# Half of an RWKV layer's operand steps made beside its recurrence instead of ahead of it

## The chip, the cores and the metric

The kernel runs on one core of one Trainium2 chip. The metric is the time of one launch in device microseconds, the median of several runs. A core has the engines PE (matrix multiply, with weight loads shown apart as PEld), DVE (vector), ACT (scalar functions), POOL (general purpose) and SP, whose queue issues every DMA of this kernel. All engines work on SBUF, 128 partitions wide; matrix products land in PSUM.

## The reference: what is computed

One inference step of a two-layer trunk over 1152 tokens (128 context tokens and 1024 latent tokens), width 1024. Layer 0 is attention, layer 1 a bidirectional RWKV-7 mixer with 16 heads of 64; each layer ends with an MLP. The change lies wholly in the RWKV mixer:

```
def rwkv_mixer(h, p, s0):
    xx = token_shift_centred(h)
    xr, xw, xk, xv, xa, xg = (h + xx * mu[n] for n in range(6))
    r = (xr @ w_rkv[0]).reshape(hs)
    k = (xk @ w_rkv[1]).reshape(hs)
    v = (xv @ w_rkv[2]).reshape(hs)
    g = jax.nn.sigmoid(xg @ g1) @ g2
    kk = (k * k_k).astype(F32)
    kk = kk * lax.rsqrt(jnp.sum(kk * kk, axis=-1, keepdims=True) + 1e-12)
    for d in range(2):
        wlog = -jax.nn.softplus(-(w0[d] + jnp.tanh(xw @ w1[d]) @ w2[d])) - 0.5
        decay = jnp.exp(-jnp.exp(wlog.astype(F32))).reshape(hs)
        a = jax.nn.sigmoid(a0[d] + (xa @ a1[d]) @ a2[d]).reshape(hs)
        kd = k * (1.0 + (a - 1.0) * k_a)
        y, sf = wkv_scan(r, decay, kd, v, kk, a, s0[:, d], reverse=(d == 1))
        bonuses.append(jnp.sum(r * kd * r_k, axis=-1, keepdims=True) * v)
...
def step(S, inp):
    r_t, w_t, k_t, v_t, kk_t, kka_t = inp
    sk = jnp.einsum('bhvk,bhk->bhv', S, kk_t)
    S = S * w_t[:, :, None, :] - sk[..., None] * kka_t[:, :, None, :] + v_t[..., None] * k_t[:, :, None, :]
    return S, jnp.einsum('bhvk,bhk->bhv', S, r_t)
```

The sum of both directions is normalised per head, the bonuses are added, the gate g is multiplied in, and w_o follows.

## The kernel before, in words

The mixer has two functions. `rwkv_proj` makes everything that is a product of the whole layer; `rwkv_scan` runs the recurrence in chunks of 64 tokens, 18 chunks per sequence, for eight pairs of heads, both directions at once.

**Projections.** The activations lie as features by tokens in three blocks of 384 columns. `lowranks` makes the first low-rank products; `dense` then runs the three dense products k, r and v, each as 8 output tiles by 3 token blocks with three matmuls per weight piece (the values are split in a high and a low half), at line 1111, from weights that `load_piece` and the halving at 1098 and 1099 (POOL for the low half `pwl`) prepare. The token mixes of the next product are made beside it (1064 to 1068).

Beside the dense products r and v, a generator `operands` (line 1243) is stepped. One operand step is one head pair and one token block, 24 in all, and makes what the recurrence reads, for each direction: two second low-rank products (`second`, line 1189, three matmuls of halves each), tanh and exponentials on ACT, a prefix sum on DVE (1277), the products `ar` (kk and r times the decays, POOL, 1285 and 1286) and `bk` (1290 on POOL, 1291 and 1293 on DVE, 1294 on POOL), stored to DRAM as `ard` and `bkd`, and the triangular products `ng` of the 32-token halves (PE, 1305, masked by DVE at 1307). At its end come the bonus terms (1313 on POOL, 1314 on DVE, `head_sums` at 1124). Its working tiles come from pool `rp2`, and, once the inputs of the dense products are used up, from the activations' pool (`etiles`). The loop steps it at every second iteration from the fifth on, so that all 24 steps are done when the projections end. The triangular matrices of a pair are inverted by `invert` (31 rounds of two DVE operations, 1364 and 1365): for the first three pairs behind their last operand step, for the others in the scan. The first two chunks of all pairs are inverted together in one run of 128 partitions.

**Pools.** When `rwkv_proj` returns, its pools (`rp1`, `rp2`, the activations and two in PSUM) are dropped and the pools of the scan take the space. A tile of the scan can so exist only once the tiles of the projections that lay there are done.

**Scan.** `rwkv_scan` builds a plan: `put` gives each generator a number of steps spread over a stretch of time units (one unit is one recurrence step), and the sorted list is the order in which instructions are emitted. A scheduler then orders each engine's instructions from a simulated timeline. The generators are `invert`; `prepare` (1428), which loads `ar`, `bk` and the triangles for six chunks, forms the chunk products `gp` (1467, one matmul of 128 weight columns by 192 columns for each head and chunk) and masks them into `g` (DVE, 1468), and joins the inverses `tt` with two small products (1483 and 1489); `recurrence` (1497), 18 steps per pair and 144 in all; and `finish` (1600), which normalises the output of a pair with tiles from a ring "f". One recurrence step on PE is `cp` (1542), then x = -cp on ACT (1550), the product of x and the inverse (1557), its copy to `mu` on ACT (1559), and the new state (1564), to which DVE adds `sd` (1567), the decayed state, that POOL makes (1548) from the state before. The outputs `yp` (1554 and 1573) run beside it.

Every operand of these PE products is written at an own `tile_position`, so that heads of 64 use halves or quarters of the array.

Of the kernel before, what the change touches and what calls it, by code (L numbers as in the profile page):

```python
# [10 lines left out]
F32 = mybir.dt.float32  # L11
# [10 lines left out]
KD = 8  # L22
# [27 lines left out]
NEK = 1  # L50
# [39 lines left out]
class Net:  # L90
# [930 lines left out]
    def rwkv_proj(self, act, early, pool, pse, ps):  # L1021
        A, S, V, G, T, dma, dr = self.A, self.S, self.V, self.G, self.T, self.dma, self.dr
        KE = (V, G)[KDE]
# [21 lines left out]
        hb = early.tile([128, 120], F32, name="hb")  # L1045
# [7 lines left out]
        vs, turn = [], 0  # L1053
# [30 lines left out]
        def load_piece(srcs):  # L1084
            raw = early.tile([128, KD, 128], F32, tag="praw", name=self.nm("praw"), bufs=1)
# [28 lines left out]
        def out32(dst, b, p):  # L1114
            o = pool.tile([128, TB], F32, tag="ro", name=self.nm("ro"), bufs=2)
# [4 lines left out]
        def head_sums(x, out):  # L1120

            sp = ps.tile([128, 3, 2], F32, tag="st", name=self.nm("hst"), bufs=1)
# [4 lines left out]
        def rows_out(out, src):  # L1127

            o, x = out.rearrange("k e (t p) -> (k e t) p", p=128), src.rearrange("p k e t -> p (k e t)")
            for i in range(0, x.shape[1], 72):  # L1130
                tp = pse.tile([128, HW], F32, tag="tp", name=self.nm("rtp"), bufs=3)[0:72, 0:128]
                T.transpose(tp, x[:, i : i + 72], self.ident)
                rt = load(None, "rt")[0:72, 0:128]
                S.copy(rt, tp)
                dma(o[i : i + 72], rt)

        def lowranks(n, hs, after):
# [12 lines left out]
            for b in range(3):  # L1150
                t = early.tile([128, TB], F32, tag="mix", name=self.nm("lt"), bufs=3)
# [10 lines left out]
                if n == 5:  # L1162
                    x = pool.tile([128, 2, TB], F32R, tag=("ar", "ar", "bk")[b], name=self.nm("lg"), bufs=2)
                    hi, lo = x[:, 0], x[:, 1]
                else:
                    hi = pool.tile([128, TB], F32R, tag="lth", name=self.nm("lth"), bufs=6)
                    lo = pool.tile([128, TB], F32R, tag="ltl", name=self.nm("ltl"), bufs=6)
                S.copy(hi, t)
                V.tensor_tensor(lo, t, f32(hi), op=ALU.subtract)
                tl[n, b] = (hi, lo)  # L1170
                after(b)

        def second_weights(n, p8):

            raw = pool.tile([128, 128], F32, tag="w2r", name=self.nm("w2r"), bufs=1)
            src = A[{1: "rwkv_w2", 4: "rwkv_a2", 5: "rwkv_g2"}[n]][0]
            dma(raw, (src if n == 5 else src.rearrange("d r n -> (d r) n"))[:, p8 * 128 : p8 * 128 + 128])
            hi = pool.tile([128, 128], F32R, tag="w2hi", name=self.nm("w2hi"), bufs=3)
            lo = pool.tile([128, 128], F32R, tag="w2lo", name=self.nm("w2lo"), bufs=3)
            S.copy(hi, raw)  # L1180
            V.tensor_tensor(lo, raw, f32(hi), op=ALU.subtract)
            return hi, lo

        def second(n, w, b, r):
            hi, lo = w
            th, tlo = tl[n, b]
            p = pse.tile([128, HW], F32, tag="lp", name=self.nm("lp"), bufs=3)[:, 0:TB]
            for j, (x, y) in enumerate(((hi, th), (hi, tlo), (lo, th))):
                T.matmul(p, x[r], y[r], start=j == 0, stop=j == 2)
# [27 lines left out]
        def v_done(p8, b, p):  # L1217
            o = out32(self.vd[:, p8], b, p)
            for c in range(0, 6, 3):
# [3 lines left out]
                vt = early.tile([128, TB], F32, tag="mix", name=self.nm("vt"), bufs=3)[0:64]  # L1223
# [669 lines left out]
```

## Time and profile before

| | us |
|---|---|
| median of three runs | 4447.08 |
| lowest and highest run | 4445.78 and 4457.35 |
| the profiled execution, device time | 4456.37 |
| its span in the trace | 4454.5 |
| busy PE, DVE, ACT, POOL in it | 3996.6, 2783.2, 1681.4, 1227.4 |

The profile is of one execution. "Busy" is the time in which an engine executes; what it waits for is inferred from semaphore events. A stage of the kernel can be told apart by cutting the span at the times at which a line first and last runs: the dense products (line 1111) end at 2710.6, the recurrence's x (line 1550) runs from 2790.8 to 3483.8, so the RWKV mixer's second half of projections and its scan fill about 2262 to 3490. Rows in the windows view give, for each stretch, the busy time of each engine with the number of instructions, then the clock that PE was granted as a share of full speed, the DMA share and GB/s.

### The profile page before, as it was taken

Reading aid. Unit: us, or ns where it says so; the run is one execution under the profiler, and the core shown is the slowest. Engines: PE = TensorE matmul, PEld = TensorE weight load, DVE = VectorE, ACT = ScalarE, POOL = GpSimd, SP = SyncE. Lnnn points to the kernel's source line nnn. Section 1 sums busy time; section 2 is a strip of 40 time slices with the busy share of each in tenths; the row PEclk is TensorE's granted clock in tenths of the full one; section 3 lists DMA queues with packets and bytes.
Section 4 is the critical chain, followed back from the end, with each engine's and each line's share of the span. In section 5 each row is a group of like instructions: output and inputs, shape, how many; then the busy total and the mean of one; then the engine's idle time right before and its main releaser. Section 6 shows DMA issues by size and latency. Waiting matters only on the chain. (4 is left out here: it accounts for less than half of the span.)

```text
span 4454.5 us, 76517 instructions
## 1 busy us (share of the span) xinstructions
PE 3996.6 (90%) x29026; PEld 3437.9 (77%) x29026; DVE 2783.2 (62%) x5866; ACT 1681.4 (38%) x3930; POOL 1227.4 (28%) x1519
## 2 busy tenths in 40 slices
PE   7989998879999999988976786989999699999998
PEld 5767776658888888868976675777777589999997
DVE  6856778865666676675248785767543564444445
ACT  5436776544211211143444453444444242222112
POOL 1223557650000000024255575434443200000001
PEclk8999999889999999989987786999999699999999
DMA  4444223232222222221334667765653511111112
GB/s 163 128 141 117 76 73 90 81 103 96 72 72 69 78 72 72 86 91 34 108 116 136 176 206 182 156 152 136 155 135 87 183 62 48 38 48 43 43 38 99
DMA packets 651182, 452.22 MB, mean 102 GB/s; under 512 B 301894, under 2 KB 606526, under 8 KB 649662
## 3 DMA queue, kind: packets, MB, share of 16 engines
q1 hardware_dynamic: 650816, 447.33, 34.9%
q8 instruction: 230, 3.77, 0.4%
q14 instruction: 136, 1.11, 0.1%
HBM read 323.45 MB, written 123.76 MB: 100 GB/s over the span
## 5 line engine op out<-in xcount | busy, mean ns | idle before, releaser
L956 PE MATMUL acc<-w2h,f 128*128 128x512 f32 x2304 | 733.7, 392 | 7.6 <-ACT f L835 5.1
L936 PE MATMUL mp<-h_b,w1h 128*128 128x384 f32 x1536 | 521.8, 340 | 0.0
L936 PE MATMUL mp<-h_a,w1h 128*128 128x384 f32 x1536 | 517.0, 337 | 0.8 <-ACT h L300 0.7
L936 PE MATMUL mp<-h_a,w1l 128*128 128x384 f32 x1536 | 517.0, 337 | 0.0
L956 PEld LDWEIGHTS acc<-w2h,f 128*128 128x128 f32 x2304 | 431.9, 188 | 104.5 <-ACT f L835 6.8
L956 PE MATMUL acc<-w2l,f 128*128 128x512 f32 x1152 | 451.3, 392 | 0.0
L962 DVE TENSOR_TENSOR acc<-acc,acc 128x1024 f32<-128x1024 f32 x270 | 329.0, 1219 | 135.5 <-PE acc L956 132.9
L660 POOL TENSOR_TENSOR ptl<-pt,pth 128x512 fp32r<-128x512 f32 x192 | 248.0, 1294 | 215.9 <-DVE pth L659 126.2
L936 PEld LDWEIGHTS mp<-h_a,w1h 128*128 128x128 f32 x1536 | 288.5, 188 | 7.0 <-issue 2.0
L936 PEld LDWEIGHTS mp<-h_b,w1h 128*128 128x128 f32 x1536 | 288.9, 188 | 4.2 <-issue 0.7
L1467 PE MATMUL gp<-ar,bk 128*128 128x192 f32 x1152 | 278.7, 372 | 14.8 <-DMA bk<-bkd 10.2
L936 PEld LDWEIGHTS mp<-h_a,w1l 128*128 128x128 f32 x1536 | 289.1, 188 | 0.1
L1111 PE MATMUL rp<-mxh,pwh 128*128 128x384 f32 (+2 forms) x720 | 267.3, 372 | 24.3 <-ACT lt L1154 7.1
L938 ACT ACTIVATE mt<-mp 128x384 f32<-128x384 f32 x192 | 94.0, 490 | 493.3 <-PE mp L936 491.6
L1111 PE MATMUL rp<-h_b,pwh 128*128 128x384 f32 (+2 forms) x720 | 263.5, 366 | 2.0 <-DVE h_b L1068 2.0
L988 POOL TENSOR_TENSOR acc<-acc,mraw 128x1024 f32<-128x1024 f32 x6 | 15.3, 2558 | 900.9 <-DVE mrv L110 894.2
L1111 PE MATMUL rp<-mxh,pwl 128*128 128x384 f32 (+2 forms) x720 | 261.9, 365 | 0.0
L956 PEld LDWEIGHTS acc<-w2l,f 128*128 128x128 f32 x1152 | 216.2, 188 | 44.7 <-issue 3.1
L1793 POOL MEMSET h_a<- 128x8 f32 x4 | 0.3, 113 | 904.3 <-PE mp L936 904.3
L940 DVE TENSOR_TENSOR mf<-mt 128x384 f32<-128x384 f32 x192 | 106.4, 554 | 212.4 <-ACT mt L938 212.3
L1468 DVE TENSOR_TENSOR g<-gp,gm 128x384 f32<-128x384 f32 x288 | 156.8, 555 | 109.9 <-PE gp L1467 98.6
L1467 PEld LDWEIGHTS gp<-ar,bk 128*128 128x128 f32 x1152 | 197.1, 204 | 31.7 <-POOL ar L1444 10.4
(452 smaller groups left out, 9584.0 us busy)
## 6 DMA issues: line engine op xcount, KB each, us to landing
mraw<-in_mlp_w_dram SPq DMA_DIRECT2D x64, 1024.0 KB
adaw<-in_w_ada_dram SPq DMA_DIRECT2D x80, 512.0 KB
bkd<-bk SPq DMA_DIRECT2D x48, 384.0 KB
ard<-ar SPq DMA_DIRECT2D x48, 384.0 KB
q<-QSd SPq DMA_DIRECT2D x256, 64.0 KB
ar<-ard SPq DMA_DIRECT2D x40, 384.0 KB
praw<-in_rwkv_w_rkv_dram SPq DMA_DIRECT2D x24, 512.0 KB
x1d<-acc SPq DMA_DIRECT2D x18, 512.0 KB
```

Of the source, the lines that this page charges most:

```text
L660: (V if w < 4 else G).tensor_tensor(c["l"][:, g : g + w, o], t["tp", g][:, 0:w], f32(c["h"][:, g : g + w, o]), op=ALU.subtract)
L936: T.matmul(p, x[:, k, :], act[b].v[y][:, k], start=k == 0 and i == 0, stop=k == KD - 1 and i == 2)
L938: S.activation(t, p, AF.Relu)
L940: V.tensor_tensor(f, t, t, op=ALU.mult)
L956: T.matmul(p[:, hf], x[:, cols], y[:, n], start=j == 0 and i == 0, stop=j == 1 and i == 2)
L962: V.tensor_tensor(a, a, pf, op=ALU.add)
L988: (G if b < 2 else V).tensor_tensor(a, a, x1[t], op=ALU.add)
L1111: T.matmul(p, x[:, k, :], a[y][:, k], start=k == 0 and i == 0, stop=k == KD - 1 and i == 2)
L1467: T.matmul(gp[:, j], x, ar[:, q + j].rearrange("p a t -> p (a t)"), start=True, stop=True)
L1468: V.tensor_tensor(g[:, e].rearrange("p j a t -> p j (a t)"), gp, gm[:, d, e, None].to_broadcast([128, 2, 192]), op=ALU.mult)
L1793: net.G.memset(a.hx[:, :, z : z + 1], 0.0)
```

## The change

The operand steps of the last four pairs leave the projections. The loop now steps `operands` at twelve listed iterations only, and `rwkv_proj` returns the generator; the scan's plan steps it for the other twelve, three for each pair, from 10 units ahead of the first recurrence step on and 24 units per pair. For this the pool `rp2` and the pool of late tiles stay open through both stages, and the operand tiles come from `rp2` alone (ten "e" tiles; `ar` and `bk` share three). A table `banks` says from which PSUM tag the operand steps take their tiles, and the scan changes it to its own tags.

```
-EB, LB, KDE, OF, BKE = 7, 4, 1, 5, 1
-PL = 13
+EB, LB, ABE, OF = 10, 4, 3, (7, 10, 13, 16, 19, 26, 29, 32, 35, 38, 42, 46)
+PL = 9
-GB = 8
-AB = 3
-GT = 22
+GB = 6
+AB = 2
+FB = 3
+GT = 18
-TTB = 5
+TTB = 4
-PI = 3
+PI = 2
+PO = 4
...
-            if i >= OF and i % 2:
+            if i in OF:
                 next(ops)
-        for _ in ops:
-            pass
-        rows_out(self.bsd, bss)
+        return ops
...
+        def made(n):
+            for _ in range(n):
+                next(ops)
+                yield
...
-        put(self.invert(pool, KD), 32, -12, 8)
+        put(self.invert(KD), 32, -6, 8)
+        put(self.invert(KD + 1), 32, 103.5, 116.5)
...
+            if p >= PO:
+                put(made(3), 3, 24 * (p - PO) - 10, 24 * (p - PO) + 14)
             if p >= PI:
-                put(self.invert(pool, p), 32, t - 45, t - 25)
+                put(self.invert(p), 32, t - 45, t - 32)
             for b in range(3):
-                put(prepare(p, b, us[p]), 16, t + 18 * b - PL, t + 18 * b - PL + 9)
+                put(prepare(p, b, us[p]), 16, t + 18 * b - PL, t + 18 * b - PL + 7)
```

Beside both stages' tiles in SBUF, rings are shorter (above: `rp`, `ar`, `g`, `tt`; the finish's "f" ring falls from five tiles to three, `sd` from two to one), prepare leads by 9 units instead of 13, the inverses of the first chunks are split in two runs of 64 partitions (four pairs each), and `tt` is 64 columns wide instead of 128. The x of a recurrence step is therefore written per head by two ACT operations into fixed tiles:

```
-                x = pool.tile([128, 2, 64], F32, tag=f"x{k}", name=self.nm("x"), bufs=1)
-                S.mul(x, cp[:, 0], -1.0)
+                x = xts[k]
+                for e in range(2):
+                    S.mul(x[row(e), e], cp[row(e), 0], -1.0)
```

The chunk products are made in two tiles of 64 weight columns, at positions (0, 0) and (0, 64):

```
-                            x = bk[e][:, q + j].rearrange("p a t -> p (a t)")
-                            T.matmul(gp[:, j], x, ar[:, q + j].rearrange("p a t -> p (a t)"), start=True, stop=True)
+                            for x in range(2):
+                                T.matmul(gp[row(x), j].rearrange("p (a t) -> p a t", t=64), bk[e][:, x, q + j], ar[:, :, q + j], start=True, stop=True, tile_position=(0, 64 * x))
```

The second low-rank products become one fp32 matmul each in place of three of halves, and the halves of the low-rank activations and weights are no longer made:

```
-            for j, (x, y) in enumerate(((hi, th), (hi, tlo), (lo, th))):
-                T.matmul(p, x[r], y[r], start=j == 0, stop=j == 2)
+            T.matmul(p, w[r], tl[n, b][r], start=True, stop=True)
```

Last, the arrays `ard`, `bkd` and `vtd` in DRAM and their tiles put the pair's two members ahead of the chunks, so that a row of one member's six chunks is 1536 bytes in one piece:

```
-        self.vtd = dr.tile([KD, 64, NC, 2, 64], F32, name="vtd")
-        self.ard = [dr.tile([KD, 128, NC, 2, 64], F32, name=f"ard{d}") for d in range(2)]
-        self.bkd = [dr.tile([KD, 128, NC, 2, 64], F32, name=f"bkd{d}") for d in range(2)]
+        self.vtd = dr.tile([KD, 64, 2, NC, 64], F32, name="vtd")
+        self.ard = [dr.tile([KD, 128, 2, NC, 64], F32, name=f"ard{d}") for d in range(2)]
+        self.bkd = [dr.tile([KD, 128, 2, NC, 64], F32, name=f"bkd{d}") for d in range(2)]
```

The first place where instructions move is PE at the seam between projections and scan. Before (lp are the second low-rank products, ng the triangles and hst the bonus sums of operand steps, rtp the transposed bonus sums, gp the first chunk product of the scan):

```order
L1305 MATMUL ng_27131<-ar_27120,bk_27127 32x32 x24
L1305 MATMUL ng_27190<-bk_27186,ar_27178 32x32 x24
L1124 MATMUL hst_27220<-ones_19676,es_27103 128x2 x3
L1305 MATMUL ng_27260<-ar_27249,bk_27256 32x32 x24
L1305 MATMUL ng_27315<-bk_27311,ar_27304 32x32 x24
L1124 MATMUL hst_27344<-ones_19676,es_27232 128x2 x3
L1132 MATMUL rtp_27354<-ident,bss 72x128
L1467 MATMUL gp_27445<-ar_27431,bk_27387 128x192 x2
```

After, at the same place (rp is the last dense product, vp its transposes, sp the first state of the recurrence, yp its first outputs):

```order
L1118 MATMUL rp_25438<-mxh_23357,pwl_25136 128x384
L1215 MATMUL vp_25466<-ident,ro_25463 64x128 x3
L1215 MATMUL vp_25473<-ident,ro_25463 64x128 x3
L1182 MATMUL lp_25558<-lt_19897,w_5009_25544 128x384
L1182 MATMUL lp_25564<-lt_20104,w_5010_25546 128x384
L1182 MATMUL lp_25616<-lt_19897,w_5009_25544 128x384
L1182 MATMUL lp_25622<-lt_20104,w_5010_25546 128x384
L1517 MATMUL sp_26032<-ident,s_5106_26029 128x64 x2
L1545 MATMUL yp_26042<-rp_25512,mu_26035 64x64
L1291 MATMUL ng_25584<-ar_25571,bk_25579 32x32 x24
```

Before, the last operand steps stood behind the last dense product; after, the thirteenth step stands among the first instructions of the scan.

The second place is POOL in the scan's first part, between the recurrence's `sd` products. Before (g is a copy into the chunk products' tile, ar with ey a decay diagonal of prepare):

```order
L1548 TENSOR_TENSOR sd_29016<-mu_28388,Dc 64x128 x2
L1494 COPY g_28986<-ar_28973 64x2x64 x2
L1494 COPY g_29021<-ar_28973 64x2x64 x2
L1494 COPY g_29056<-ar_28973 64x2x64 x2
L1548 TENSOR_TENSOR sd_28625<-mu_28074,Dc 64x128 x2
L1444 TENSOR_TENSOR ar_29493<-ey,Dc 128x6x64
L1548 TENSOR_TENSOR sd_29140<-mu_29084,Dc 64x128 x2
```

After (the products ar, kd and bk of 128x384 belong to a made operand step):

```order
L1538 TENSOR_TENSOR sd_27406<-mu_27278,Dc 64x128 x2
L1271 TENSOR_TENSOR ar_27434<-kk_27413,ec_27418 128x384
L1272 TENSOR_TENSOR ar_27434<-r_27415,ec_27418 128x384
L1276 TENSOR_TENSOR kd_27438<-kd_27438,k_27411 128x384
L1538 TENSOR_TENSOR sd_27665<-mu_27278,Dc 64x128 x2
L1260 MEMSET ec_27474 128x6
L1280 TENSOR_TENSOR bk_27442<-kd_27438,en_27430 128x384
L1271 TENSOR_TENSOR ar_27490<-kk_27413,ec_27474 128x384
L1272 TENSOR_TENSOR ar_27490<-r_27415,ec_27474 128x384
L1276 TENSOR_TENSOR kd_27494<-kd_27494,k_27411 128x384
L1280 TENSOR_TENSOR bk_27498<-kd_27494,en_27486 128x384
```

Here three to six products of an operand step stand between one `sd` and the next (the last row is followed by one more, at 1299, and then by the next `sd`), where small copies stood. In the whole order, the thirteenth step's first products stand right behind the last dense one, and the twenty-fourth step is done when 45 of the 144 recurrence steps have been issued.

More of the change, by code (lines that the diff above doesn't have):

```diff
@@ L1052, in rwkv_proj, with bank @@
         tl = {}
-        vs, turn = [], 0
+        vs = []
+        self.banks = dict(tp=(pse, "tp", 3), lp=(pse, "lp", 3), st=(ps, "st", 1), ng=(ps, "ng", 1))
+        def bank(what, shape):
+            p, tag, bufs = self.banks[what]
+            return p.tile(shape, F32, tag=tag, name=self.nm(what), bufs=bufs)
         def mix(n, b):
@@ L1120, in head_sums @@
         def head_sums(x, out):
-            sp = ps.tile([128, 3, 2], F32, tag="st", name=self.nm("hst"), bufs=1)
+            sp = bank("st", [128, 3, 2])
             for t in range(3):
@@ L1129, in rows_out @@
             o, x = out.rearrange("k e (t p) -> (k e t) p", p=128), src.rearrange("p k e t -> p (k e t)")
[L1130 to L1133, printed above, removed]
+            n = min(x.shape[1], 72)
+            for i in range(0, x.shape[1], n):
+                tp = bank("tp", [128, HW])[0:n, 0:128]
+                T.transpose(tp, x[:, i : i + n], self.ident)
+                rt = load(None, "rt")[0:n, 0:128]
                 S.copy(rt, tp)
-                dma(o[i : i + 72], rt)
+                dma(o[i : i + n], rt)
         def lowranks(n, hs, after):
@@ L1161, in lowranks @@
                     V.tensor_scalar(t, t, 0.5, 0.5, op0=ALU.mult, op1=ALU.add)
[L1162 to L1170, printed above, removed]
+                tl[n, b] = t
                 after(b)
         def second_weights(n, p8):
-            raw = pool.tile([128, 128], F32, tag="w2r", name=self.nm("w2r"), bufs=1)
+            w = pool.tile([128, 128], F32, tag="w2", name=self.nm("w2"), bufs=3)
             src = A[{1: "rwkv_w2", 4: "rwkv_a2", 5: "rwkv_g2"}[n]][0]
[L1177 to L1182, printed above, removed]
-        def second(n, w, b, r):
-            hi, lo = w
-            th, tlo = tl[n, b]
-            p = pse.tile([128, HW], F32, tag="lp", name=self.nm("lp"), bufs=3)[:, 0:TB]
-            for j, (x, y) in enumerate(((hi, th), (hi, tlo), (lo, th))):
-                T.matmul(p, x[r], y[r], start=j == 0, stop=j == 2)
+            dma(w, (src if n == 5 else src.rearrange("d r n -> (d r) n"))[:, p8 * 128 : p8 * 128 + 128])
+            return w
+        def second(n, w, b, r):
+            p = bank("lp", [128, HW])[:, 0:TB]
+            T.matmul(p, w[r], tl[n, b][r], start=True, stop=True)
             return p
@@ L1251, in operands @@
             self.tri = {}
-            ndp = self.tri[KD] = dr.tile([KD, 2, 2, 2, 2, 32, 32], F32, name="ndp")
+            for i in range(2):
+                self.tri[KD + i] = dr.tile([KD // 2, 2, 2, 2, 2, 32, 32], F32, name=f"ndp{i}")
             for p8 in range(KD):
@@ L1317, in operands @@
                         self.tri[p8] = nd
+                        rows_out(self.bsd[p8 : p8 + 1], bss[:, p8 : p8 + 1])
                         if p8 < PI:
-                            for _ in self.invert(pool, p8):
+                            for _ in self.invert(p8):
                                 pass
@@ L1387, in rwkv_scan @@
         row = lambda e: slice(64 * e, 64 * e + 64)
-        bks = [[pool.tile([128, NB, 2, 64], F32, name=f"bk{i}{e}") for e in range(2)] for i in range(2)]
+        bks = [[pool.tile([128, 2, NB, 64], F32, name=f"bk{i}{e}") for e in range(2)] for i in range(2)]
         for i in range(2):
@@ L1807, in body @@
         P.drop("tacc", "tm", "traw", "tpt")
-        pool, ps = P.add("rp2"), P.add("rpp2", "right", PSUM)
-        net.rwkv_proj(hs, early, pool, pse, ps)
-        P.drop("rp2", "rp1", "act", "rpp1", "rpp2")
-        late, psl = P.add("scl", "right"), P.add("scpl", "right", PSUM)
+        late, ps = P.add("scl", "right"), P.add("rpp2", "right", PSUM)
+        net.inv_pool = P.add("rp2", "right")
+        ops = net.rwkv_proj(hs, early, net.inv_pool, late, pse, ps)
+        P.drop("rp1", "act", "rpp1", "rpp2")
+        psl = P.add("scpl", "right", PSUM)
         pool, ps = P.add("sc"), P.add("scp", space=PSUM)
-        last = net.rwkv_scan(pool, late, ps, psl)
-        P.drop("sc", "scp")
+        last = net.rwkv_scan(pool, late, ps, psl, ops)
+        P.drop("sc", "scp", "rp2")
         net.act_pool = P.add("act")
```

125 lines of the change are left out of this document (60 added, 65 removed).

## Prediction

> **What bounds the kernel now.** I read the windows view first, cut at the stages of the odd layer: the second half of the projections (2262 to 2755), the start of the scan, the scan's first 46 recurrence steps, and the rest. Columns: stretch, length, busy us of PE, PEld, DVE, ACT, POOL, clock, DMA share, GB/s.
>
> ```profile
> 2262.00:2755.00 493.00, 373.40 (x3964) 328.86 (x3963) 339.19 (x507) 227.67 (x505) 294.97 (x297) 0.80 0.57 171
> 2755.00:2790.00 35.00, 22.34 (x162) 17.36 (x162) 21.90 (x55) 5.79 (x18) 15.70 (x32) 0.60 1.02 179
> 2790.00:3030.00 240.00, 223.81 (x3209) 180.97 (x3209) 164.46 (x443) 108.14 (x339) 96.25 (x234) 0.95 0.70 149
> 3030.00:3490.00 460.00, 414.27 (x6049) 333.97 (x6050) 222.79 (x589) 189.91 (x619) 182.35 (x421) 0.89 0.51 123
> 2262.00:2350.00 88.00, 81.02 (x691) 74.61 (x691) 29.75 (x38) 29.78 (x63) 43.63 (x41) 0.91 0.51 150
> ```
>
> The scan is PE's: 93% in its first part, 90% in the rest. The projections are PE's while few operand steps run (81 of 88 us, 92%), but over their second half PE is busy only 76%. The sources of the last dense product and of the recurrence's x place the seam, and the length of the whole:
>
> ```profile
> span 4454.5 us, 76517 instructions
> L1111 PE MATMUL rp<-mxh,pwl x720: 332/338/687, 1983.2 to 2710.6; 128*128 128x384 f32 x144, 128*128 128x386 f32 x24, 128*128 128x388 f32 x12
> L1550 ACT ACTIVATE x<-cp x144: 262/278/295, 2790.8 to 3483.8; 128x128 f32<-128x128 f32 x144
> ```
>
> From 2711 to 2791 neither dense product nor recurrence runs. What holds the second half is seen in the timeline of DVE and POOL (start, duration, line):
>
> ```profile
> 2727.20 0.55 DVE L1291 SCALAR_TENSOR_TENSOR es<-es,kk 128x384 f32<-128x384 f32 x1
> 2727.66 0.61 DVE L1314 SCALAR_TENSOR_TENSOR es<-r,CB,es 128x384 f32<-128x384 f32 x1
> 2728.19 0.97 DVE L1277 TENSOR_TENSOR_SCAN es<-m,es 128x390 f32<-128x390 f32 x1
> 2733.63 1.04 DVE L1291 SCALAR_TENSOR_TENSOR tha<-tha,kk 128x384 f32<-128x384 f32 x1 [2.19 <-ACT kd L1289]
> ```
>
> ```profile
> 2721.87 1.00 POOL L1290 TENSOR_TENSOR es<-es,k 128x384 f32<-128x384 f32 x1 [0.46 <-ACT es L1289]
> 2732.47 0.92 POOL L1286 TENSOR_TENSOR ar<-r,es 128x384 f32<-128x384 f32 x1
> 2734.20 1.26 POOL L1286 TENSOR_TENSOR ar<-r,ec 128x384 f32<-128x384 f32 x1
> 2748.75 0.85 POOL L1294 TENSOR_TENSOR bk<-es 128x384 f32<-128x384 f32 x1
> 2749.58 0.98 POOL L1313 TENSOR_TENSOR es<-es,es 128x384 f32<-128x384 f32 x1
> ```
>
> L1291 takes 0.55 while POOL is idle and 1.04 beside a POOL operation; L1286 takes 0.92 alone and 1.26 beside DVE. So I count the two engines as taking turns. One operand step, alone: DVE 2 x (0.97 + 0.55 + 0.55, the last taken for L1293 as for L1291) + 2 x 0.61 (L1314, and the product kk at L1262 taken like it) = 5.4; POOL 2 x (0.92 + 0.92 + 1.00 + 0.85) + 0.98 = 8.4; together 13.8 us. The groups of the projections' second half, and below them two of the scan's first part, give the other work of this kind (busy, mean ns):
>
> ```profile
> L1365 DVE TENSOR_TENSOR iv<-iv,ivt 128x31 f32<-128x31 f32 (+15 forms) x93 | 54.2, 582 | 1.6
> L1099 POOL TENSOR_TENSOR pwl<-praw,pwh 128x1024 fp32r<-128x1024 f32 x14 | 34.5, 2466 | 17.4 <-ACT pwh L1098 15.5 <-PE ng L1305 1.9
> L1064 POOL TENSOR_TENSOR nbr<-h_a 128x384 f32<-128x384 f32 (+2 forms) x22 | 21.3, 979 | 18.2 <-DVE mix L1066 18.2
> L1068 DVE TENSOR_TENSOR h_b<-mix,mxh 128x384 fp32r<-128x384 f32 x24 | 18.7, 791 | 0.0
> L1066 DVE SCALAR_TENSOR_TENSOR mix<-nbr,hb,mix 128x384 f32<-128x384 f32 x21 | 16.6, 797 | 1.3 <-POOL nbr L1064 0.9 <-ACT mix L1065 0.4
> ...
> L1365 DVE TENSOR_TENSOR iv<-iv,ivt 128x231 f32<-128x231 f32 (+15 forms) x106 | 39.8, 376 | 2.3
> L1364 DVE TENSOR_TENSOR ivt<-iv 128x240 f32<-128x240 f32 (+15 forms) x105 | 38.4, 366 | 3.5 <-DMA iv<-in_c_eye_dram 1.4
> ```
>
> Sum: 24 x 13.8 = 331; the 2 x 93 inverse operations at 0.37 as in the scan, 69; pwl 34; the three mixing groups 57, of which I take two thirds (estimate, since they are stretched too), 38. That is 472 of 493 us, 96%. This pair, not PE, bounds the stretch.
>
> **The change part by part.** All terms are in the profiled execution (4456.4; span 4454.5), which lies 9.3 above the median of the runs.
>
> *Projections with 12 operand steps.* The pair: 12 x 13.8 = 166, 211 inverse operations (by the new order) x 0.37 = 78, 34 and 38: 316, at 96% 329 us. PE, for the check:
>
> ```profile
> L1189 PE MATMUL lp<-lth,w2hi 64*128 64x384 f32 x96 | 34.8, 484 | 11.5 <-ACT cum L1275 7.9 <-ACT es L1275 2.8 <-ACT ro L1116 0.8
> L1189 PE MATMUL lp<-lth,w2lo 64*128 64x384 f32 x96 | 27.9, 387 | 4.1 <-DVE w2lo L1181 4.1
> L1189 PE MATMUL lp<-ltl,w2hi 64*128 64x384 f32 x96 | 27.3, 379 | 0.0
> L1305 PE MATMUL ng<-ar,bk 64*32 64x32 f32 x1152 | 18.2, 217 | 29.4 <-DVE bk L1293 22.3 <-DVE es L1307 4.3 <-DVE nt L1307 2.9
> L1305 PE MATMUL ng<-bk,ar 64*32 64x32 f32 x1152 | 16.8, 210 | 23.6 <-DVE bk L1293 13.8 <-DVE es L1307 9.2 <-POOL ar L1286 0.6
> L1124 PE MATMUL hst<-ones,es 128*128 128x2 f32 x90 | 16.0, 292 | 25.1 <-DVE es L1314 21.9 <-DVE bss L1125 3.0
> L1611 PE MATMUL fq<-y,cm 128*128 128x384 f32 x42 | 18.7, 527 | 0.0
> ```
>
> A step costs PE now (90.0 + 35.0 + 16.0) / 24 = 5.9. Its four low-rank products, three matmuls each, become four fp32 products of two records like L1611's: 4 x 1.05 = 4.2, with ng 1.5 and hst 0.7 a step of 6.3. So 373 - 24 x 5.9 + 12 x 6.3 = 308, at the 92% of the first window 334. Both limits lie close together and will cost a little more jointly: I take 338, a gain of **-155**. Bounds: at today's 76%, 405 (-88); at 95%, 323 (-170). The gates' products change from three matmuls of 0.34 to one of 1.05: nothing.
>
> *Scan with 12 operand steps.* By PE: 224 + 12 x 6.3 + about 8 us of shape changes between the steps' products and the scan's (estimate: some 7 a step at 0.09, below), 308 at 93%, 331: +91. By the pair: POOL 96, inverses 78, 12 x 13.8 = 166, 340 at 96%, 354: +114. The scan's own DVE work reads PSUM and isn't counted (its main product g keeps one duration throughout, row below at the small terms). I take **+100**, 8.3 us a step. Bounds: +66, when PE fills every idle moment (224 + 76 + 6 = 306), and +190, if a step costs 16 us because POOL's in-order queue holds the recurrence's `sd` behind three to six operand products. On SP's queue each made step puts its loads and stores ahead of prepare's loads; I cost that at nothing, under cover of a DMA share of 0.70 over 240 us.
>
> *Shape changes on PE.*
>
> ```profile
> 2903.27 0.92 PE L1467 MATMUL gp<-ar,bk 128*128 128x192 f32 x4
> 2904.11 0.31 PE L1483 MATMUL mp<-ta,g 32*32 32x32 f32 x6
> ```
>
> ```profile
> 2906.68 1.57 PE L1467 MATMUL gp<-ar,bk 128*128 128x192 f32 x8
> 2908.18 0.37 PE L1489 MATMUL mp<-tt,z 32*32 32x32 f32 x10
> 2908.48 0.69 PE L1557 MATMUL cp<-x,tt 128*64 128x64 f32 x16
> 2909.09 0.43 PE L1489 MATMUL mp<-tt,z 32*32 32x32 f32 x14
> ```
>
> Four gp records hold PE 0.84 until the next group, eight hold it 1.50: 0.165 each, and 0.18 for entering and leaving, 0.09 a change. Counted in the orders, changes among gp, mp and the recurrence fall from 763 to 412, since gp now has the recurrence's 64-column shape: 351 x 0.09 = 32, half of it on the path: **-16** (-32 to 0).
>
> *gp in two column tiles.* Twice as many records, half as wide. The 16 records of 64 columns above, alternating between two column tiles, take 0.61, 0.038 each; a third of gp's 0.165 is 0.055. Half of that, 0.0275, would be tiles wholly side by side, and 0.01 remains per record. For gp that makes 2304 x (0.0825 + 0.01) = 213 for 1152 x 0.165 = 190 today, some of it covered: **+18**. Bounds 0 and +72 (2304 x 0.165 x 0.69 = 262, if the ratio of 0.69 holds for wide ones). The Trainium skill, "TensorEngine Tiling (Array Packing)", Tiling Modes, says that different tiles execute LdWeights and Matmul in parallel, and that changing the mode drains TensorE. The second agrees with the 0.09 above; by the first this term would be 0 and my forecast 18 lower.
>
> *Small terms.* The x of a step becomes two ACT operations: 144 more of about 0.24, below the 262 of L1550's shortest, 35 us, a quarter of it on the chain between cp and cp: **+9** (0 to +35). The finish ring shrinks from five tiles to three. Three rows of the sources: the durations of g, then POOL's idle time (us, times) before the finish's product with v (L1635) and before the recurrence's `sd` (L1548):
>
> ```profile
> L1468 DVE TENSOR_TENSOR g<-gp,gm x288: 536/558/560, 2766.9 to 3419.2; 128x384 f32<-128x384 f32 x144
> ```
>
> ```profile
>   DMA v<-vd: 57.2, 16
> ```
>
> ```profile
>   DVE mu L1567: 141.3, 69
> ```
>
> With fewer tiles the load is issued later, and POOL also serves the recurrence: **+5** (0 to +45, nearly that idle time doubled). Rows of 1536 bytes in place of 256 or 512 ease the start of the scan, where the DMA share is 1.02: **-5** (-10 to 0).
>
> **Sum:** -155 + 100 - 16 + 18 + 9 + 5 - 5 = -44: 4412 in the profiled execution's terms, less 9.3, **4403 us**. Its own range, from terms half way to their bounds, is 4350 to 4440.
>
> **The rivals.** *The scan swallows the steps.* PE has 16 idle us in the first part and 46 in the rest; DVE and POOL are under 70%. All terms at their good end: -170 + 66 - 32 - 10 = -146, **4301**. Against it: PE at 93% hardly ever reaches 98. Chance 0.12.
>
> *Nothing comes of it.* Wide column tiles keep the ratio of 0.69: +72 in place of +18 takes -44 to +10, **4457**. For it: the one measured ratio. Against it: it comes from records so short that a fixed part weighs most. Chance 0.15.
>
> *Slower: the steps stand in the recurrence's way.* In-order POOL and DVE run a step's 13.8 us while `sd` and the recurrence's sum wait behind them, and PE, whose other scan work is limited by prepare's shorter lead, idles. Without the +100 the sum is -144, so from 12.0 us a step on the kernel is slower; at 13.8 it is +22, **4469**, and at 13.8 x 1.3, the stretch seen when both engines run, +72, 4519. For it: POOL's `sd` is already in step with the recurrence (141.3 us of waiting for its sum), and the projections show that the pair stretches. Against it: g, in PSUM on one side, shows no stretch (536 to 560 ns). Chance 0.20.
>
> The Trainium skill, "SBUF — State Buffer", SBUF: two separate sides, calls the port pair of these engines an exclusive lock, held for a whole instruction by a DVE operation with two SBUF inputs or by GpSimd. The 1.04 and 1.26 fit that; nothing here shows who is served first.
>
> **How the numbers follow.** Forecast 0.53, the rivals as given. Differences under 0.3%, 13 us, can't be told from none. Faster: 0.53 + 0.12 = 0.65; same 0.15; slower 0.20. The range reaches from the first rival, 4300, to just above the third at 13.8, 4475; its stretched end is left out.
>
> **What would show it.** The last dense product near 2555 to 2600 (2711 before) and the first x about 80 later; the 46th x some 340 after the first (240 now); gp records with less than 0.1 between starts when in groups; DVE and POOL over 60% beside the first half of the recurrence. The forecast is wrong if the projections stay near 76% PE, if `sd` waits in POOL's queue show as PE idle before cp or yp of over 5 us a made step, or if gp's groups take 1.4 times as long.

## The result, and the profile after

The changed kernel takes 4590.5 us (median of four runs, 4588.6 to 4590.8) against 4451.1 for the kernel before beside it: a ratio of 1.0312, 95% interval 1.0294 to 1.0330. It is 139 us slower; the forecast was 4403.

The span, the last dense product and the recurrence's x in the source view of the changed kernel answer to the rows shown of before (2710.6 for the dense product, 2790.8 to 3483.8 for x, span 4454.5):

```profile
span 4589.0 us, 78674 instructions
L1118 PE MATMUL rp<-mxh,pwl x720: 331/338/694, 1988.6 to 2631.2; 128*128 128x384 f32 x144, 128*128 128x386 f32 x24, 128*128 128x388 f32 x12
L1541 ACT ACTIVATE xt<-cp x288: 252/272/278, 2691.5 to 3631.4; 64x128 f32<-64x128 f32 x144
```

The recurrence begins 99 us earlier (2691.5 against 2790.8), as the change says. But from first to last x it now takes 940 us instead of 693, 247 more. What follows the last x is 13 us shorter. -99 + 247 - 13 = 135, the difference of the two spans. So the whole loss is in the scan. The made steps' last products run at 3109, and the 46th recurrence step begins at 3110. The first 46 recurrence steps take 425 us against 246, the other 98 take 514 against 447. So 179 us are lost beside the made steps, and 68 after the last of them.

The windows view of the changed kernel: the projections while few steps run, their second half, the seam, the first part of the scan (the first 46 recurrence steps end at 3117), and the whole scan:

```profile
2262.00:2350.00 88.00, 75.01 (x650) 67.72 (x650) 24.91 (x38) 29.31 (x61) 39.18 (x37) 0.86 0.51 145
2262.00:2631.00 369.00, 289.23 (x2546) 259.21 (x2546) 223.28 (x379) 152.14 (x323) 177.27 (x167) 0.85 0.54 148
2631.00:2691.00 60.00, 30.37 (x340) 19.26 (x338) 42.75 (x91) 20.17 (x49) 22.07 (x39) 0.68 0.64 168
2691.00:3090.00 399.00, 290.85 (x4288) 220.25 (x4288) 246.97 (x543) 166.00 (x471) 182.57 (x309) 0.70 0.55 138
2691.00:3635.00 944.00, 750.76 (x11561) 580.16 (x11561) 490.67 (x1171) 402.97 (x1247) 391.30 (x776) 0.78 0.51 128
```

Beside the made steps PE is busy 73% where it was 93%, at a granted clock of 0.70 where it was 0.95. DVE and POOL are busy 62% and 46%: neither is full. So no engine is the limit here; the recurrence waits, and what PE does it does at a lower clock.

### The profile page after: what moved, and what is told of

It is laid out like the page before. It is cut to its first block, busy times and chain, and to the rows that moved or that the text cites. A ratio compares the mean times of both kernels' runs of the same rounds, so it can differ in the third digit from the quotient of the medians.

```text
span 4589.0 us, 78674 instructions
## 1 busy us (share of the span) xinstructions
PE 4040.0 (88%) x30064; PEld 3435.6 (75%) x30064; DVE 2776.5 (61%) x5895; ACT 1719.1 (37%) x4050; POOL 1226.8 (27%) x1517
## 5 line engine op out<-in xcount | busy, mean ns | idle before, releaser
L1457 PE MATMUL gp<-ar,bk 128*64 128x192 f32 x2304 | 303.6, 380 | 54.5 <-DVE g L1458 35.9
L1457 PEld LDWEIGHTS gp<-ar,bk 128*64 128x64 f32 x2304 | 187.1, 158 | 85.9 <-DVE g L1458 44.2
```

The costliest lines, as they stand in the source:

```text
L1457: T.matmul(gp[row(x), j].rearrange("p (a t) -> p a t", t=64), bk[e][:, x, q + j], ar[:, :, q + j], start=True, stop=True, tile_position=(0 ...
```

## The experiments

Each kernel ran beside the kernel before on the same chip. Ratios are to that run of before, with their 95% intervals; times are medians.

**All steps back in the projections.** The edit to the changed kernel:

```
-OF = (7, 10, 13, 16, 19, 26, 29, 32, 35, 38, 42, 46)
+OF = tuple(range(5, 48, 2))
...
+        for _ in ops:
+            pass
         return ops
...
-                put(made(3), 3, 24 * (p - PO) - 10, 24 * (p - PO) + 14)
```

> The changed kernel with all 24 operand steps back in the projections and none in the scan; rings, layouts, gp tiles, the two x operations and the plan stay as changed. Theory S (the steps made in the scan stand in the recurrence's way): the scan is as fast as before, 693 us from first to last x within 20, and the time is 4430 to 4465. Rival R (shorter rings and prepare's shorter lead slow the scan with or without steps): the changed kernel's last 98 recurrence steps, none of them beside a made step, took 541 us where the kernel before took 453, 0.9 us a step more; over 144 steps that is 130 us, so the scan takes about 820 and the time is about 4570. Rival F (the new form of gp and x costs it): the same as R here.

Measured: 4603.1 us, ratio 1.0340 (1.0318 to 1.0362). Its source view:

```profile
L1118 PE MATMUL rp<-mxh,pwl x720: 331/338/673, 1990.8 to 2865.9; 128*128 128x384 f32 x144, 128*128 128x386 f32 x24, 128*128 128x388 f32 x12
L1543 ACT ACTIVATE xt<-cp x288: 269/272/276, 2948.7 to 3646.3; 64x128 f32<-64x128 f32 x144
```

and its scan in the windows view, to be set beside the last row of the changed kernel above:

```profile
2948.00:3650.00 702.00, 612.38 (x10305) 484.68 (x10301) 321.39 (x835) 328.18 (x1087) 275.33 (x654) 0.90 0.49 124
```

The scan takes 698 us: by this number S is right about the scan, R and F are not. (The 541 us that the expectation builds R on start at 3090, ahead of the end of the made steps; from the 47th x on it is 514 against 447.) The scan of the changed kernel is 940 - 698 = 242 us longer, 20.2 for each of the twelve steps. But the time isn't that of before, which no theory had: with the same 24 steps as before the first x comes at 2949 instead of 2791. In this form of the kernel a step costs (2949 - 2691) / 12 = 21.5 us in the projections too. So moving the steps is worth about nothing, and what slowed the kernel is spread over both stages.

The two runs differ in more than the steps, which both prices hide. The rounds of the inverses in the scan, in this run and then in the changed kernel:

```profile
L1353 DVE TENSOR_TENSOR iv<-iv,ivt 64x252 f32<-64x252 f32 (+23 forms) x80 | 29.9, 374 | 1.5
```

```profile
L1351 DVE TENSOR_TENSOR iv<-iv,ivt 128x87 f32<-128x87 f32 (+21 forms) x186 | 81.5, 438 | 3.8
```

Here 106 rounds that the changed kernel makes in its scan have run in the projections (the scan of before has 176). So 20.2 us is an upper price of a step in the scan, and 21.5 one in the projections; a run further below that keeps the inverses in the scan gives 16.2 for the first. There are two questions from here: what makes a step cost 16 to 20 us in the scan, and what made the projections slow.

**The parts of the change alone, in the kernel before.** Rings and lead as in the change, with the finish ring at three tiles instead of five, one `sd` tile instead of two, and the windows for the later inverses and for prepare at 13 and 7 units instead of 20 and 9:

```
-GB, AB, GT, TTB, PL = 8, 3, 22, 5, 13
+GB, AB, GT, TTB, PL = 6, 2, 18, 4, 9
```

> The kernel before with only the room taken away as in the change: GB 6, AB 2, GT 18, TTB 4, finish ring 3, sd one tile, prepare's lead 9 over 7 units, inverse window 13. Theory S and rival F: within 15 us of before (4451). Rival R: 60 to 130 us slower, 4510 to 4580.

Measured: 4492.7, ratio 1.0095 (1.0069 to 1.0120), +42 us; x runs from 2790.5 to 3523.3, all of it in the scan. Less than R's 60 to 130 and more than the 15 of S and F, but eight times my term for the finish ring, and I had no term for the other rings.

gp in two tiles:

```
-T.matmul(gp[:, j], x, ar[:, q + j].rearrange("p a t -> p (a t)"), ...)
+for x in range(2):
+    T.matmul(gp[row(x), j], bk[e][:, q + j, x], ar[:, q + j]..., tile_position=(0, 64 * x))
```

> The kernel before with only the chunk products gp made in two tiles of 64 weight columns. My sum had +18 for the tiles and -16 for fewer shape changes: 4453, within 15 of before. Rival F: the records keep the ratio of 0.69 and gp holds PE 72 us longer, 4500 to 4525; or, if the shape changes matter more than I took, faster by up to 30.

Measured: 4465.1, ratio 1.0030 (1.0018 to 1.0042), +14. Its gp over the scan, and the scan's window; then the same two of before:

```profile
L1467 PE MATMUL gp<-ar,bk 128*64 128x192 f32 x2192 | 283.0, 357 | 19.8 <-DVE g L1468 17.2 <-issue 1.9 <-DMA bk<-bkd 0.5
```

```profile
2788.00:3500.00 712.00, 620.30 (x10344) 490.48 (x10341) 385.12 (x1028) 295.00 (x955) 278.81 (x655) 0.90 0.57 130
```

```profile
L1467 PE MATMUL gp<-ar,bk 128*128 128x192 f32 x1101 | 261.4, 366 | 1.6 <-DVE g L1468 1.6
```

```profile
2790.00:3488.00 698.00, 636.65 (x9255) 514.66 (x9255) 387.25 (x1031) 297.32 (x955) 278.60 (x655) 0.91 0.58 132
```

Both of my PE terms show: gp is busy 22 us longer, and PE as a whole 16 us less, so by difference the shape changes saved more than I took. Yet the scan takes 708 us, 15 more: PE now idles before gp, 17 us of it for DVE's g, where it idled 2 before. At those places PE isn't what ends last. A term priced on PE alone didn't pass into the time.

x in two operations:

```
-S.mul(x, cp[:, 0], -1.0)
+for e in range(2):
+    S.mul(x[row(e)], cp[row(e), 0], -1.0)
```

> The kernel before with only the recurrence's x written by two ACT operations of 64 partitions instead of one of 128. My sum: +9, 4460. Upper bound: +35, 4486, if the second operation lies wholly on the chain from cp to cp.

Measured: 4462.9, ratio 1.0024 (1.0009 to 1.0038), +12 for my +9.

**What a made step waits for in the scan.** First sd on DVE, by one switch (SD 0 to 1) of the changed kernel.

> The changed kernel with the recurrence's sd made on DVE instead of POOL, so that no product of a made operand step on POOL stands ahead of it. Known by now: with all steps in the projections the scan takes 697 us, with twelve in it 940, 20 us a step. Theory P (sd behind three to six POOL products is what holds the recurrence): the scan falls by 60 to 120 us, time 4470 to 4530. Rival T (a made step costs its own latency: twelve working tiles a step from a ring of ten, so that steps run one after the other and the recurrence waits for what hangs on them): within 20 us of the changed kernel, 4570 to 4610. Slower than that if DVE's queue is the longer one.

Measured: 4587.3, ratio 1.0309 (1.0291 to 1.0326): no change. That alone would leave open whether DVE's queue is as long, but in the changed kernel's own trace hardly anything of the recurrence waits for `sd`: the copy `mu` on ACT 6.3 us, `cp` on PE 0.5. POOL's queue ahead of `sd` is not the cause; theory P falls.

Steps further apart in the plan (24 to 33 units a pair):

> The changed kernel with the made steps 11 units apart in the plan instead of 8, so that they lie beside 66 more percent of... the same twelve steps beside about 130 recurrence units instead of 96. If a step has a fixed price (theories P and T), the scan stays at 940 within 20 us, 4570 to 4610. If the price is the crowding of steps that can't start before the last one's tiles are free, the scan falls by 40 to 100 us, 4490 to 4550.

Measured: 4577.1, ratio 1.0293 (1.0277 to 1.0308), 9 to 13 us better, with intervals that overlap; the scan takes 938. So the price hardly depends on how close the steps lie to each other.

Steps in pieces: three yields in each half step (ahead of ar, ahead of the triangles, behind their store), and the plan takes 21 pieces a pair over the same 24 units:

```
+                        yield
...
-            for _ in range(n):
+            for _ in range(7 * n):
...
-                put(made(3), 3, 24 * (p - PO) - 10, 24 * (p - PO) + 14)
+                put(made(3), 21, 24 * (p - PO) - 10, 24 * (p - PO) + 14)
```

> The changed kernel with each made step cut into seven pieces that the plan puts 1.1 units apart, in place of one lump; the steps in the projections are unchanged. Theory Q (the lump stands in program order ahead of recurrence and prepare on the in-order queues of PE, POOL and DVE, and they wait for its chain): the scan falls by 50 to 120 us, 4470 to 4540. Rival T: within 20 us, 4570 to 4610.

Measured: 4523.3, ratio 1.0171 (1.0155 to 1.0186), 67 us less than the changed kernel; the scan takes 867 (14.1 us a step instead of 20.2). The order of the same instructions on the queues is a third of the price: Q holds for that part. Its scan in the windows view:

```profile
2693.00:3565.00 872.00, 716.89 (x11538) 552.87 (x11530) 489.88 (x1169) 403.81 (x1244) 395.99 (x773) 0.83 0.55 138
```

The timelines of PE and DVE in the changed kernel show how it works (start, duration, line, idle time before it):

```profile
2848.52 0.45 PE L1555 MATMUL cp<-mu,g 128*64 128x64 f32 x8
2848.80 0.40 PE L1564 MATMUL yp<-g,mu 128*64 128x64 f32 x6
2850.14 0.66 PE L1291 MATMUL ng<-ar,bk 64*32 64x32 f32 x48 [0.94 <-DVE bk L1279]
2850.75 0.37 PE L1532 MATMUL cp<-mu,g 128*64 128x64 f32 x1
```

```profile
2848.07 0.74 DVE L1277 SCALAR_TENSOR_TENSOR tha<-tha,kk 128x384 f32<-128x384 f32 x1 [1.71 <-ACT kd L1275]
2848.84 1.16 DVE L1279 SCALAR_TENSOR_TENSOR bk<-tha,en 128x384 f32<-128x384 f32 x1
2849.92 0.60 DVE L1558 TENSOR_TENSOR mu<-cp,sd 64x128 f32<-64x128 f32 x2
```

The recurrence's cp ends at 2848.97. Its sum mu stands on DVE behind the step's tha and bk and starts at 2849.92, 0.95 us late. On PE the next cp stands behind ng, which waits for the same bk. The waits of the first part of the scan (us, times, longest), in the changed kernel and then with the steps in pieces, name the three places:

```profile
DVE kk L1249 <- DMA kk<-kkd: 45.8, 10, 6.7
PE ng L1291 <- DVE bk L1279: 25.6, 10, 9.0
PE gp L1457 <- DVE g L1458: 22.5, 11, 6.3
```

```profile
DVE kk L1249 <- DMA kk<-kkd: 38.0, 9, 10.5
PE gp L1461 <- DVE g L1462: 20.8, 17, 5.0
PE ng L1293 <- DVE bk L1280: 7.6, 3, 7.0
```

In pieces, PE stands at ng for 7.6 us instead of 25.6. DVE still stands at a step's first product for the load of kk, 38 us in nine stops, and gp's waits for g are as long as they were. The Trainium skill, "TensorE: Matmul & The Clock Gate", in its table of specs, gives ScalarE, VectorE and GpSimdE strict first-in first-out queues; that is what these rows show of DVE.

A fifth load tile (LB 4 to 5, GT 18 to 17 for the room), in the changed kernel and in the one with pieces:

> The changed kernel with five instead of four tiles for the loads k, kk and r of the operand steps (one g tile fewer for the room). With four, the load of the next step's kk can only be issued when the last step lets go of a tile, and DVE stands at its first product (45.8 us idle in ten stops in the scan's first 399 us) with g and the recurrence's sums queued behind it. Theory K (this stop is a large part of a made step's price): 25 to 50 us faster than the changed kernel, 4540 to 4565. Rival: the recurrence waits elsewhere in that time anyway, within 15 us of 4590.

> The fifth load tile together with the made steps cut into seven pieces (4523 by itself). Theory K: 20 to 45 us more come off, 4480 to 4505, since the cut alone left 38 us of DVE standing at kk. Rival: the cut has already taken what the fifth tile can give, 4510 to 4530.

Measured: 4572.7, ratio 1.0275 (1.0258 to 1.0293), some 17 us less than the changed kernel; but 4557.5, ratio 1.0238 (1.0214 to 1.0261), with the pieces, some 30 us more than the pieces alone. By itself the tile gives less than K's 25 and a little more than the rival's 15; in the combination it loses, which neither had. Why isn't shown. The fifth load tile also costs a g tile, and the scheduler makes another order from the same plan as soon as a ring changes; I put the loss down to that order, which is argued, not tried. Gains of this size in the scan don't add.

**What slowed the projections.** The activations' tiles for three of four half steps, first with 12 steps in the projections, then with 24:

```
+turn = (turn + 1) % 4 if len(vs) == 3 and self.inproj else 0
+if turn:
+    t = self.act_pool.tile([128, KD * HW], F32, tag=f"acta{turn - 1}", ...)
```

> The changed kernel with three of four half steps in the projections taking their six tiles from the activations' pool again, as before the change; the made steps in the scan are unchanged. With the ring of ten alone, twelve more steps in the projections cost 235 us by the last dense product (2866 against 2631), 19.6 each; the engines' turns were 13.8. Theory T: the last dense product comes 30 to 70 us earlier, time 4520 to 4560. Theory P, or any that puts the cost on the engines and not on tiles: within 15 us of 4590.

> All 24 operand steps in the projections as in the earlier run (4603), but with the tiles of the activations' pool for three of four half steps, as in the kernel before; everything else as changed. If the tile supply alone made that run's projections slow: the last dense product at 2710 to 2740 in place of 2866 and the first x near 2800, scan 697, time 4450 to 4475. If the new layouts, the shared ar and bk ring or the fp32 products cost the projections something themselves: 4500 to 4560.

Measured: 4569.8, ratio 1.0272 (1.0257 to 1.0287), and 4554.4, ratio 1.0231 (1.0213 to 1.0250). With 24 steps the first x moves from 2949 to 2887, 62 us; with 12 it hardly moves (2688) where T wanted 30 to 70 us, and the gain of 20 is in the scan, whose instructions are the same. So T fails with 12 steps, holds with 24, where the ring is crowded, and leaves 96 us open. With these tiles, moving the steps *costs*: 1.0272 with twelve in the scan, 1.0231 with none.

The shared ring and the fp32 products (with the making of the halves left out), each alone in the kernel before:

```
-ar = pool.tile(..., tag="ar", ..., bufs=2)     bk = pool.tile(..., tag="bk", ..., bufs=2)
+ar = pool.tile(..., tag="ab", ..., bufs=3)     bk = pool.tile(..., tag="ab", ..., bufs=3)
```

```
-for j, (x, y) in enumerate(((hi, th), (hi, tlo), (lo, th))):
-    T.matmul(p, x[r], y[r], start=j == 0, stop=j == 2)
+T.matmul(p, w[r], tl[n, b][r], start=True, stop=True)
```

> The kernel before with only one thing changed: ar and bk of the operand steps share a ring of three tiles instead of two each. With all steps in the projections and the activations' tiles given back, the changed kernel still starts its recurrence at 2886 instead of 2791. Theory A (a half step needs one ar and one bk; with three tiles the next half step's bk waits for a store to DRAM): 30 to 90 us slower than before, 4480 to 4540. Rival: the ring isn't what holds it, within 15 us of 4451.

> The kernel before with only the second low-rank products made by one fp32 matmul instead of three of halves, without the halves' making. My sum had nothing for it (three matmuls of 0.34 against two records of 0.53): within 10 us of 4451. Rival: the fp32 records hold PE longer between the dense product's, or the freed ACT and DVE work helps the pair: 15 to 40 us either way.

Measured: 4474.0, ratio 1.0053 (1.0035 to 1.0072), and 4472.0, ratio 1.0047 (1.0031 to 1.0062): +26 and +24. Each starts x at 2800.9, 10 us late; the rest is in the scan. Neither was in my sum as a loss. The shared ring lies between theory A's 30 to 90 and its rival's 15; the fp32 products lie in their rival's band. Four shared tiles in the changed kernel, with one e tile and one g tile fewer, and the same with all steps in the projections:

> The changed kernel with four shared tiles for ar and bk instead of three (one e tile and one g tile fewer for the room). Theory A: both the projections and the made steps gain, 30 to 70 us, 4520 to 4560. Rival (the made steps are held by the recurrence's and the steps' places in the in-order queues, not by this ring): within 15 us of 4590.

> All 24 steps in the projections, with the activations' tiles and four shared ar and bk tiles. Theory A: the first x near 2800 instead of 2886, scan 695 to 710, time 4450 to 4480. Rival: the first x stays within 20 us of 2886, and what else was changed in the projections (two inverse runs of 64 partitions instead of one of 128, the order that follows from them) costs the rest: 4540 to 4560.

Measured: 4596.8, ratio 1.0325 (1.0301 to 1.0349), no change, and 4566.4, ratio 1.0254 (1.0235 to 1.0273), with x from 2884.9. Theory A isn't borne out: beside the other shortages the fourth tile, paid for with an e tile and a g tile, gives nothing. The groups of the run with activations' tiles and 24 steps, up to the seam, point elsewhere:

```profile
L1364 DVE TENSOR_TENSOR ivt<-iv 128x31 f32<-128x31 f32 (+25 forms) x178 | 93.9, 528 | 29.3 <-DMA iv<-in_c_eye_dram 15.6 <-DMA iv<-nd 10.1
L1365 DVE TENSOR_TENSOR iv<-iv,ivt 128x31 f32<-128x31 f32 (+25 forms) x178 | 102.4, 575 | 3.8
```

That is 178 rounds of inverses, where before had 93: the operand pool lives on, so the scan's inverses no longer wait for the scan's pool and run ahead, on one of the two engines that I took to bound this stretch. Closing the pool and giving the inverses room in the scan's pool:

```
-        P.drop("rp1", "act", "rpp1", "rpp2")
+        P.drop("rp2", "rp1", "act", "rpp1", "rpp2")
...
+        net.inv_pool = pool
```

> All 24 steps in the projections with the activations' tiles and four shared ar and bk tiles (4566 in the earlier run), but the operand pool closed at the projections' end as before the change and the scan's inverses with their tiles in the scan's pool, so that none of them can run ahead. In the earlier run six inverses ran before the first x (2885) where the kernel before ran three, and DVE, half of the pair that bounds the projections, had some 80 us more work there. Theory H: that is the rest of the projections' delay; the first x comes at 2800 to 2830, time 4480 to 4510. Rival: the first x stays at 2870 to 2890 and the time at 4550 to 4570; then the fp32 products and layouts hold the projections.

Measured: 4540.4, ratio 1.0193 (1.0166 to 1.0220). x runs from 2833.4 to 3578.8: it starts 52 us earlier than without the hold, and the scan takes 23 us longer with the inverses in it (239 rounds instead of 124). H holds for half of the delay, just behind the 2800 to 2830 that it claimed; 42 us stay, of which the fp32 products are 10 by themselves.

This run also gives a second measure of a made step. Its scan has no made step, more rounds of the inverses than the changed kernel's, and takes 745 us: by it the steps cost 940 - 745 = 195 us, 16.2 each. Its last 98 recurrence steps take 501 us, so most of what the changed kernel loses there (514) comes without any made step; I take it for the inverses and the shorter rings, which isn't tried by itself.

**All gains together**, and the layouts alone:

> All that helped, together: made steps cut into seven pieces and 11 units apart, the fifth load tile, and the activations' tiles for the steps in the projections. If the gains add up (67 + 13 + 30 + 20), 4455 to 4470, no faster than the kernel before; below 4435 if the pieces also let PE keep its clock. The price of a made step would then be about 10 to 14 us in the scan against 8.6 in the projections with those tiles (12 steps moved the first x from 2791 to 2688), so that moving them still doesn't pay.

Measured: 4518.0, ratio 1.0150 (1.0127 to 1.0174). The gains don't add (the expectation had 4455 to 4470), and the kernel stays slower than before; the price of a step in its scan is (876 - 698) / 12 = 15 us, by the same upper measure as 20.2.

The layouts in the kernel before (ard, bkd, vtd and all their tiles), with gp in two tiles, everything else as before:

```
-self.ard = [dr.tile([KD, 128, NC, 2, 64], ...)]      ar = pool.tile([128, NB, 2, 64], ...)
+self.ard = [dr.tile([KD, 128, 2, NC, 64], ...)]      ar = pool.tile([128, 2, NB, 64], ...)
```

> The kernel before with only the layouts of ard, bkd, vtd and their tiles changed (rows of 1536 bytes), and gp in two column tiles, without which the weights' layout can't be read; gp in two tiles alone took 4465. My sum had -5 for the longer rows: 4460. If fewer descriptors matter for the projections' stores and the scan's start (DMA share 1.02 there): 4430 to 4450, and this would be the fastest version. If the strided reads on PE cost: above 4475.

Measured: 4431.9 us, ratio 0.9953 (0.9937 to 0.9970): faster than both kernels, and 0.8% faster than gp in two tiles alone. Its x in the source view, and the packets of the whole run in its page and in that of before:

```profile
L1551 ACT ACTIVATE x<-cp x144: 270/277/297, 2791.3 to 3465.9; 128x128 f32<-128x128 f32 x144
```

```profile
DMA packets 558522, 452.39 MB, mean 102 GB/s; under 512 B 191302, under 2 KB 529214, under 8 KB 556990
```

```profile
DMA packets 651182, 452.22 MB, mean 102 GB/s; under 512 B 301894, under 2 KB 606526, under 8 KB 649662
```

The start is unchanged (2791.3); the scan takes 675 instead of 693, and 708 with gp's tiles alone. So the long rows pay in the scan, and not where the DMA share was 1.02. How they pay isn't shown: the two longest waits for loads in the scan, those for ta and v, sum to 158 us here and 166 with gp's tiles alone, which is little beside 33. This was the best part of the change, and I had it at -5.

## Why the prediction was wrong

- **The step that failed is the scan with 12 operand steps:** "I take +100, 8.3 us a step". Measured are 242, 20.2 a step, against the run with none in the scan, and 195, 16.2 a step, against the one that also keeps the inverses there: either is above my bound of 190. I priced a step by what it adds to the busiest engines: 6.3 us of PE, or 13.8 of the pair's turns. What PE did in the two scans (944 and 702 us of window) splits the 242: PE's busy time rose from 612 to 751, 138 us, and its idle time from 90 to 193, 104 us. Of the 138, 75 are the steps' own products, as priced; the other 63 are the products that both scans have, at a lower clock, 0.78 against 0.90. Two neighbouring stretches of the changed kernel's scan, and gp in each, show what the clock does:

```profile
2929.00:2953.00 24.00, 17.59 (x362) 13.33 (x358) 11.44 (x25) 13.63 (x43) 16.77 (x29) 1.00 0.67 187
2953.00:2976.90 23.90, 21.86 (x263) 14.99 (x263) 8.45 (x16) 11.11 (x34) 7.80 (x15) 0.50 0.40 89
```

```profile
L1457 PE MATMUL gp<-ar,bk 128*64 128x192 f32 x70 | 7.8, 337 | 0.0
L1457 PE MATMUL gp<-ar,bk 128*64 128x192 f32 x16 | 3.1, 539 | 0.2 <-issue 0.2
```

  At clock 1.00 gp holds PE 0.11 us a record, at 0.50 it holds it 0.19. Over the whole scans gp's records last 333 ns on the mean at full clock and some 525 at half, with the made steps and without them, so the steps don't lengthen them in another way. So by the upper measure a step is 6.3 us of its own work, 5.2 of everyone's work at a lower clock and 8.6 of idling; with the steps in pieces it is 6.3, 2.4 and 5.5. My price had next to nothing for the last two.
- The Trainium skill, "TensorE: Matmul & The Clock Gate", Part 1, says that a monitor gates PE's clock by how busy it has been lately, at half rate after an idle window. The rows agree in kind: 0.95 at 93% busy in the scan's first part before, 0.70 at 73% after.
- **The slower rival had the sign and a part of the mechanism.** It said that steps stand in the recurrence's way on in-order queues and decides from 12.0 us a step; its stretched price, 13.8 x 1.3 = 17.9, lies within the measured 16 to 20. Of its two places one was wrong: POOL's `sd` is innocent. The recurrence's sum on DVE does wait, and the queue that it didn't name is PE's, at ng. A third of the price goes when the same instructions are queued in pieces. What idling then stays is not taken apart further. I gave this rival 0.20; the row for it that I passed over is the step's own chain from ACT to DVE to PE, which in the projections already ended PE's waits ("PE MATMUL ng ... 29.4 <-DVE bk L1293 22.3").
- **The projections term** (-155) was priced at 13 us a step. PE stays 78% busy in the second half (289 of 369 us), where my sum had 91% and I had called staying near 76% a sign of being wrong. Twelve steps more cost 21.5 each in the new form, with 106 rounds of inverses that come with them; with the activations' tiles, and 52 rounds fewer, they cost 12.1 (2833 against 2688), so the price of a step there isn't settled. But the new form also starts 158 us later with all 24 steps. Of that the runs show 62 for the activations' tiles and 52 for inverses that run ahead; 10 each from the fp32 products and the shared ring alone; some 25 are open. Net the first x gained 99 where I had 155. I had named the tile supply in the diff and given it no price.
- **The small terms:** rings +42 where I had +5; the fp32 products +24 and the shared ring +26 where I had nothing; x +12 for +9; gp and shape changes +14 for +2, with PE's own time as I had it; layouts about -33 for -5. Signs were right for all that I priced, sizes only where an operation lay on the recurrence's chain. The parts run alone sum to 42 + 14 + 12 + 24 + 26 - 33 = +85, with the inverses that run ahead (26) to 111; with all steps in the projections and the activations' tiles the changed kernel is 1.0231, +103. That these come close proves little, since other parts didn't add.
- **The whole miss:** the sum was -44, the spans differ by +135, 179 us more. Of these 142 are the made steps in the scan (242 for 100) and 56 the start (-99 for -155); the rest goes 20 the other way, 13 of it behind the last x.

## What to carry to other kernels

A chain of work put beside a recurrence costs more than its busy time: it costs what waits behind each of its instructions on every engine's queue, and, once PE idles, a lower clock for everything else. Price these too, and cut the chain into pieces before judging the idea. A run that takes the work out again is a clean measure only if nothing else moves with it: here the inverses did. When stages are made to overlap, price the room first: here shorter rings, a smaller tile supply and work that may suddenly run ahead cost more than the seam was worth. And run the helpers of a change alone: the long rows, made only to fit the rest, were the one part that gained.

## What the runs showed of the hardware

PE's busy time isn't a property of the kernel's matmuls: the same scan work with steps beside it filled some 63 us more at a mean granted clock of 0.78 instead of 0.90. In these traces the granted clock is either 1.00 or 0.50, in stretches of 3.4 us and more, and a mean between them is a mix of the two. And two column tiles of 64 with 192 moving columns hold PE only 8% longer than one of 128 (283 against 261 us for the scan's gp, in windows with 2192 and 1101 records), so here they run side by side almost wholly.
